# The up stage of a ConvFFN in seven products: halves cut at whole blocks, halo columns in four of the seven, and the second half of the first two tiles moved to the end

## The chip, the cores and the metric

The kernel runs on one core of a Trainium2 chip. A core has five engines with queues of their own: PE (matrix products, with PEld for its weight loads), DVE (vector), ACT (scalar functions), POOL (a second vector engine) and SP, which here only issues DMA transfers. They meet through semaphores. The metric is the device time of one launch in microseconds (us), the median of several runs. The kernel before takes 1351.69 us.

## The reference

One decoder layer for one sequence of 1024 tokens, with 16 meta tokens ahead of it and a width of 1024:

```
a = rmsnorm(h, ln_mix_pre);  proj = a @ w_in
y = concat(diff_attention(...), hgrn2(...))          # both read proj
h = h + rmsnorm(y @ w_out, ln_mix_post)
a = rmsnorm(h, ln_ffn_pre)
u = causal depthwise conv of width 3 over tokens (a @ w_up) + bias     # 1024 -> 2 * 2816
y = (gelu(u[:, :2816]) * u[:, 2816:]) @ w_down                         # 2816 -> 1024
h = h + rmsnorm(y, ln_ffn_post)                       # meta tokens dropped
```

All of it is fp32. The change lies between the output projection (`@ w_out`) and the down projection (`@ w_down`), in the product `a @ w_up`, called the up stage here.

## The kernel before, in words

A product in fp32 is made of three matmuls on split operands: every matrix is written as a high part (a cast) plus a low part (the rest, by a subtraction), and hi·hi, hi·lo and lo·hi are summed in PSUM. For the weights the cast is ACT's (`uh`) and the subtraction DVE's or POOL's (`ul`); for the activations ACT casts and DVE subtracts (`t`, in `t_split`).

**Output projection.** Tokens come in nine blocks: block 0 holds two meta tokens, blocks 1 to 8 hold 128 tokens each. Per block, SP loads the mixed heads (`mp`), PE projects, `post_a` and `post_b` do the norm and the residual (`xh`), and the FFN's normed input (`a2s`) comes out. `trans` turns a finished block by PE transposes and ACT copies it into `at2`, which holds `a2s` transposed: features on partitions, tokens along the free axis. At some blocks the loop also issues work for the up stage: `prep_plain` loads the weights of feature tile 0 and splits them, `t_split` splits quarters of `at2`.

**Up stage.** Output features come in 22 gate and 22 up tiles of 128; a feature tile here is the pair. The tokens are cut in two halves (`p` = 0 and 1), and each half in two columns of 258 (half 0) or 256 (half 1). The two more columns per half are the halo of the convolution: half 0 covers 516 columns, half 1 covers 512 from column 514 on, so that two columns are computed twice, and the convolution gives 514 and 510. For one feature tile and one half, gate and up, two quarters of the inner dimension and two columns make a 2x2 block product. `plain_unit` computes it with eight block products (96 matmuls); `unit` uses the Strassen-Winograd scheme: seven products of 12 matmuls, on sums of weight quarters (`w_sum` on POOL, `prep`) and sums of activation quarters (`t_sums` on DVE, in place in `at2`). In `unit`, products 0 and 4 go to bank `pa`, products 1, 3 and 5 to `pb`, products 2 and 6 to `pc`. Between them DVE adds the banks: `u2` is read from `pb` after product 1, and product 3 may go on in `pb` only then; `u3` is read after product 3, and `uu`, `ug` are the results. `conv` does the convolution (one ACT step and two DVE steps, `c0` for the gate and `c1` for the up side), `gated` the gelu on ACT and the product on POOL, and SP stores it to DRAM (`gsc`).

Feature tile 0 is done by `plain_unit`, half 0 and then half 1, so that PE has work before the sums of `at2` exist; tiles 1 to 21 follow with `unit`, both halves of a product one behind the other, so that a product is two groups of 12 matmuls. While a tile runs, the weights of the next are loaded and split (`prep(7 * (ft + 1) + j)` at step `j`).

**Down stage.** It reads `gsc` back (`gi`, split into `gh` on ACT and `gl` on DVE) and its own weights (`wi`, into `wh` and `wl`). A part of its first loads and splits is already issued in the up stage.

**Order.** PE's order is set by hand. On the other engines a scheduler orders the instructions ahead of time, and each engine works through its list strictly in that order: an instruction that waits holds up all behind it on that engine. The three lists shown with the change are such lists.

## Time and profile before

| what | before |
| --- | --- |
| median of 3 runs (lowest to highest) | 1351.69 us (1351.08 to 1352.4) |
| the profiled execution | 1352.21 us |
| its span, first to last instruction | 1350.4 us |
| mean granted TensorE clock | 0.991 |
| busy: PE / DVE / ACT / POOL | 1293.5 / 923.6 / 688.0 / 421.1 us |
| first matmul of the up stage | 661.7 us |
| first matmul of feature tile 1 | 694.7 us |
| first matmul of the down stage | 1128.25 us |

Rows of groups give line, engine, operation, names (out<-in), shapes, count, then busy time and mean duration of one, then the idle time of that engine just before and who ended it. L53 is the line of a helper through which all DVE and ACT operations go, so there one goes by the names. Rows of the timeline give start, length, engine and instruction. Rows of stretches give for each engine the busy time and the count of instructions in it.

### The profile page before, as it was taken

The numbers are of one execution on the slowest core, as the hardware profiler recorded it, in microseconds if no ns is written. First come the engines' busy times: TensorE is split into PE (matmuls) and PEld (weight loads), VectorE is DVE, ScalarE is ACT, GpSimd is POOL, SyncE is SP. The second block draws the span as 40 slices with busy tenths as digits, with TensorE's granted clock in tenths as the row PEclk, the third lists the DMA queues.
The fourth block names the chain that finished last, engine by engine and source line by source line (L and its number), as shares of the span: only waits on it lengthen the run. The fifth ranks groups of instructions, "written<-read, shape, count | busy, mean of one in ns | idle before, by whom it ended". The sixth has DMA issues, their size and how long they took to land.

```text
span 1350.4 us, 26183 instructions
## 1 busy us (share of the span) xinstructions
PE 1293.5 (96%) x10170; PEld 1194.3 (88%) x10170; DVE 923.6 (68%) x1597; ACT 688.0 (51%) x1625; POOL 421.1 (31%) x330
## 2 busy tenths in 40 slices
PE   6999999999999998999888999999999999999997
PEld 5898999989998998777688999999999998888885
DVE  7565657574747465736897777777877876597586
ACT  7365346535654565446674444544444444554454
POOL 3211211021112110111556656666566641010021
PEclk9999999999999999999999999999999999999999
DMA  6331232133211004626612222223222225965353
GB/s 213 106 131 53 103 125 103 44 127 102 102 37 48 19 29 121 209 78 213 232 40 87 94 71 71 94 71 108 89 71 74 92 72 171 343 211 159 100 202 117
DMA packets 84082, 153.06 MB, mean 113 GB/s; under 512 B 9539, under 2 KB 22627, under 8 KB 83958
## 3 DMA queue, kind: packets, MB, share of 16 engines
q1 hardware_dynamic: 83958, 151.39, 33.7%
q8 instruction: 80, 1.31, 0.4%
q14 instruction: 44, 0.36, 0.1%
HBM read 112.69 MB, written 38.67 MB: 112 GB/s over the span
## 4 chain that ended last, share of the span: by engine, by line
PE 68%; DVE 8%; ACT 4%; DMA 3%; issue 3%; POOL 1%; SPq 1%; DVEq 0%; ACTq 0%; POOLq 0%
PE pd L1449 5%; PE pd L1450 5%; PE pd L1448 5%; PE pb L1289 4%; PE pb L1290 4%; PE pb L1291 4%; PE pa L1289 3%; PE pa L1290 3%; PE pa L1291 3%; PE pc L1289 3%; PE pc L1291 3%; PE pc L1290 3%; PE pa L704 2%; PE py L964 2%; PE py L968 2%
## 5 line engine op out<-in xcount | busy, mean ns | idle before, releaser
L1289 PE MATMUL pb<-t,uh 128*128 128x258 f32 x504 | 144.4, 286 | 8.0 <-DVE u L53 8.0
L1290 PE MATMUL pb<-t,uh 128*128 128x258 f32 x504 | 143.4, 285 | 0.0
L1291 PE MATMUL pb<-t,ul 128*128 128x258 f32 x504 | 143.0, 284 | 0.0
L1449 PE MATMUL pd<-wl,gh 128*128 128x512 f32 x308 | 121.1, 393 | 0.5 <-DVE wl L53 0.5
L1450 PE MATMUL pd<-wh,gl 128*128 128x512 f32 x308 | 121.2, 393 | 0.0
L1448 PE MATMUL pd<-wh,gh 128*128 128x512 f32 x308 | 119.7, 388 | 0.0
L53 DVE SCALAR_TENSOR_TENSOR c<-uu,cwt,c 128x514 f32<-128x514 f32 (+1 forms) x88 | 96.3, 1095 | 20.6 <-ACT c L53 19.9
L1289 PEld LDWEIGHTS pb<-t,uh 128*128 128x128 f32 x504 | 96.3, 191 | 9.4 <-DVE u L53 8.8
L1256 POOL TENSOR_TENSOR c<-c,c 128x514 f32<-128x514 f32 (+1 forms) x44 | 63.4, 1441 | 121.9 <-ACT c L53 117.8
L1290 PEld LDWEIGHTS pb<-t,uh 128*128 128x128 f32 x504 | 96.9, 192 | 0.0
L1291 PEld LDWEIGHTS pb<-t,ul 128*128 128x128 f32 x504 | 96.7, 192 | 0.0
L1289 PE MATMUL pc<-t,uh 128*128 128x258 f32 (+1 forms) x336 | 95.1, 283 | 0.0
L1289 PE MATMUL pa<-t,uh 128*128 128x258 f32 (+1 forms) x336 | 94.7, 282 | 0.0
L1290 PE MATMUL pa<-t,uh 128*128 128x258 f32 (+1 forms) x336 | 94.7, 282 | 0.0
L1291 PE MATMUL pc<-t,ul 128*128 128x258 f32 (+1 forms) x336 | 94.5, 281 | 0.0
L1290 PE MATMUL pc<-t,uh 128*128 128x258 f32 (+1 forms) x336 | 94.5, 281 | 0.0
L1291 PE MATMUL pa<-t,ul 128*128 128x258 f32 (+1 forms) x336 | 94.4, 281 | 0.0
L53 DVE SCALAR_TENSOR_TENSOR c<-ug,cwt,c 128x514 f32<-128x514 f32 (+1 forms) x88 | 86.1, 978 | 2.6 <-ACT c L53 2.0
L155 POOL TENSOR_TENSOR ul<-ws,uh 128x512 fp32r<-128x512 f32 x42 | 59.9, 1427 | 48.2 <-ACT uh L53 44.0
L1449 PEld LDWEIGHTS pd<-wl,gh 128*128 128x128 f32 x308 | 57.8, 188 | 14.8 <-DVE wl L53 1.7
L53 ACT CAST uh<-ra 128x512 fp32r<-128x512 f32 x67 | 41.2, 616 | 56.1 <-PE pb L1290 36.2
L1448 PEld LDWEIGHTS pd<-wh,gh 128*128 128x128 f32 x308 | 57.8, 188 | 13.0
(394 smaller groups left out, 4162.8 us busy)
## 6 DMA issues: line engine op xcount, KB each, us to landing
ra<-in_wup_dram SPq DMA_DIRECT2D x88, 256.0 KB, 2.7
wd<-in_wdown_dram SPq DMA_DIRECT2D x44, 256.0 KB, 4.6
tsc<-wd SPq DMA_DIRECT2D x44, 256.0 KB, 3.2
...
```

Source lines behind the costliest of these rows:

```text
L53: ins = call(*args, **kw)
L155: (eng or G).tensor_tensor(lo, raw, hi.bitcast(F32), op=ALU.subtract)
L704: T.matmul(po[:, :P], w_, vn[:, j], start=(j == 0), stop=(j == i))
L964: T.matmul(py[:r], mh[:, j, :r], hi, start=(first and j == 0), stop=False)
L968: T.matmul(py[:r], ml[:, j, :r], hi, start=False, stop=(last and k == k1 - 1))
L1256: G.tensor_tensor(cg, cg, cu, op=ALU.mult)
L1289: T.matmul(pt, hi[:, s], th[:, k], start=(first and k == 0), stop=False, skip_group_check=True)
L1290: T.matmul(pt, hi[:, s], tl[:, k], start=False, stop=False, skip_group_check=True)
L1291: T.matmul(pt, lo[:, s], th[:, k], start=False, stop=(k == 3), skip_group_check=True)
L1448: T.matmul(py, gh[:, s], wh, start=(k == 0 and pr not in (3, 7)), stop=False, skip_group_check=True)
L1449: T.matmul(py, gh[:, s], wl, start=False, stop=False, skip_group_check=True)
L1450: T.matmul(py, gl[:, s], wh, start=False, stop=(k == NH - 1), skip_group_check=True)
```

## The change

**Halves.** Both halves now have 2 x 256 columns of whole blocks (`HALF`), and half 0 has two more at its left (`EDGE`): the two halo tokens of block 0. So no block straddles the halves, and `trans` has one ACT copy for each half of a block's features where a straddling block had two. The two halo columns lie only in the left column of half 0, and thus in products 0, 1, 4 and 5; products 2, 3 and 6 have 256 columns in both halves. Half 1 has no halo: `conv` copies the last two columns of the half before to the left edge of `ug` and `uu` (two small ACT copies per feature tile), and every convolution has 512 columns.

**Order of tiles.** `PLAN` lists the slots: only half 0 of tile 0 is done by `plain_unit`; then half 0 of tile 1 alone (slot 0); tiles 2 to 21 with both halves (slots 1 to 20); and at the end half 1 of tile 0 (slot 21) and of tile 1 (slot 22), for which the weights are loaded, summed and split once more, with all low parts on DVE. Names in the up stage now carry the slot: `u2_1_0` is slot 1, half 0, and belongs to tile 2, `u2_21_1` is slot 21, half 1. The outputs carry the tile (`uu21_1`).

**Earlier.** `prep_plain` is issued ahead of the projection's loop (it was at block 6), `prep(0)` and two splits at block 5, two more at block 6, the sums of half 0 at block 7. Block 8's transposes and the splits and sums of half 1 are issued step by step in slot 0 (`second`).

**Addresses.** The convolution's buffers lie elsewhere, padding tiles have other sizes, the two pools for split weights change parity, and the early steps of the down stage are taken in another order of k.

```diff
-WN = [258, 256]
-C0 = [0, 514]
+HALF = 256
+EDGE = [2, 0]
...
-        where.tile([P, n], F32, tag="lineup", name=f"lineup{len(lined)}", bufs=1)
+        where.tile([P, n], F32, tag=f"lineup{len(lined)}", name=f"lineup{len(lined)}", bufs=1)
...
+    line_up(ep, 48)
...
-        at2.append(a2p.tile([P, KD, 2 * WN[p]], F32, tag=f"at2_{p}", name=f"at2_{p}"))
+        at2.append(a2p.tile([P, KD, 2 * HALF + EDGE[p]], F32, tag=f"at2_{p}", name=f"at2_{p}"))
...
+        p, n = divmod(max(i - 1, 0), 4)
+        c = EDGE[p] + P * n if i else 0
...
-                        at2[p][:, ks, lo_ - C0[p]:hi_ - C0[p]], pv[:, :, lo_ - cs.start:hi_ - cs.start])
+            A.copy(at2[p][:, 4 * half:4 * half + 4, c:c + r], pt[:, : 4 * r].rearrange("p (k t) -> p k t", k=4))
...
+    def width(p, j):
+        return HALF + (EDGE[p] if j in (0, 1, 4, 5) else 0)
+
+    def t_split(p, j, src, where, tag, step=None):
+        n = width(p, j)
+        step = step or n
+        both = where.tile([P, 8, step], F32R, tag=tag, name=f"t{p}_{j}")
+        hi, lo = both[:, 0:4, :n], both[:, 4:8, :n]
+        o = n - src.shape[-1]
+        A.copy(hi[:, :, o:], src)
+        V.tensor_tensor(lo[:, :, o:], src, hi[:, :, o:].bitcast(F32), op=ALU.subtract)
+        if o:
+            for a, b in zip((hi, lo), tt[p][0]):
+                A.copy(a[:, :, :o], b[:, :, :o].bitcast(F32))
         tt[p][j] = (hi, lo)
...
+    def t_sums(p):
...
-        t_split(p, 1, b22, where, f"t{p}_1")
-        t_split(p, 2, b11, where, f"t{p}_2")
-        t_split(p, 3, b12, where, f"t{p}_3")
         V.tensor_tensor(b21, b21, b22, op=ALU.subtract)
-        t_split(p, 5, b21, *last)
...
+        if EDGE[p]:
+            e1, e2 = (at2[p][:, k0:k0 + 4, :EDGE[p]] for k0 in (0, 4))
+            V.tensor_tensor(e2, e2, e1, op=ALU.subtract)
...
+    PLAN = [(1, (0,))] + [(ft, (0, 1)) for ft in range(2, NF)] + [(0, (1,)), (1, (1,))]
...
-        ft, j = divmod(q, 7)
-        if ft >= NF:
+        s, j = divmod(q, 7)
+        if s >= len(PLAN):
...
-            load_raw4(ft)
+            load_raw4(PLAN[s][0], s)
...
-        where = swp if q % 2 else wp
+        where = wp if q % 2 else swp
...
-        split(hi, lo, src, G if j % 2 == 0 and j else V)
+        split(hi, lo, src, G if j % 2 == 0 and j and s < len(PLAN) - 2 else V)
...
+    prep_plain()
...
+        if i == 5:
+            prep(0)
+            t_split(0, 0, quarter(0, 0), ep, "e0")
+            t_split(0, 4, quarter(0, 4), ep, "e1")
         if i == 6:
-            prep_plain()
-        if i == 8:
             t_split(0, 7, quarter(0, 7), mxp, "mix0", 272)
             t_split(0, 6, quarter(0, 6), mxp, "mix1", 384)
+        if i == 7:
+            t_sums(0)
         post_a(i, py)
-        if i == 4:
-            t_split(0, 0, quarter(0, 0), ep, "e0")
-            t_split(0, 4, quarter(0, 4), ep, "e1")
     post_b(8)
...
-    line_up(xup, 16)
+    line_up(xup, 8)
+    v_cm, cv = pool("conv", 2)
...
+    edges = xup.tile([P, 2, 2, 2], F32, tag="edges", name="edges", bufs=1)
...
     def conv(ft, p, side, u):
         m = ft + NF * side
-        w = 2 * WN[p] - 2
-        c = cv.tile([P, 514], F32, tag=f"c{side}", name=f"c{side}_{ft}_{p}", bufs=2 if side else 3)[:, :w]
+        w = 2 * HALF
+        if p:
+            A.copy(u[:, :2], edges[:, ft, side] if ft < 2 else last[side][:, w:])
+        else:
+            last[side] = u
+            if ft < 2:
+                A.copy(edges[:, ft, side], u[:, w:])
+        c = cv.tile([P, w], F32, tag=f"c{side}", name=f"c{side}_{ft}_{p}", bufs=2 if side else 3)
...
-        SY.dma_start(gsc[P * ft: P * (ft + 1), C0[p]:C0[p] + 2 * WN[p] - 2], cg)
...
+        SY.dma_start(gsc[P * ft: P * (ft + 1), 2 * HALF * p:2 * HALF * (p + 1)], cg)
...
+    def plain_unit(bank):
+        us = outputs(0, 0)
         for col in range(2):
+            a = 0 if col == 0 else 2 + HALF
+            n = HALF + (2 if col == 0 else 0)
...
-    def unit(ft, p, bank):
-        n = WN[p]
...
+    def unit(s_, p, bank):
+        ft = PLAN[s_][0]
...
-            hi, lo = made[7 * ft + j]
+            hi, lo = made[7 * s_ + j]
             th, tl = tt[p][j]
+            pt = pt[:, HALF + e - width(p, j):]
...
+        V.tensor_tensor(u2, pb[:, e:], x1[:, e:], op=ALU.add)
...
+        V.tensor_tensor(u3, pb[:, e:], x1[:, e:], op=ALU.add)
+        V.tensor_tensor(uu[:, 2 + HALF:], pc[:, e:], u3, op=ALU.add)
...
+        A.copy(ug[:, 2 - e:2 + HALF], pa)
...
+        V.tensor_tensor(ug[:, 2 + HALF:], pc[:, e:], u2, op=ALU.add)
         gated(ft, p, ug, uu)
...
-    p0 = plain_unit(0, lambda nm: free.pop(0))
+    p0 = plain_unit(lambda nm: free.pop(0))
     next(p0)
     trans(7)
-    t_split(1, 0, quarter(1, 0), tp, "t1_0")
-    t_split(1, 4, quarter(1, 4), tp, "t1_4")
-    for _ in range(3):
-        next(p0)
-    trans(8)
-    t_split(1, 7, quarter(1, 7), tp, "t1_5")
-    t_split(1, 6, quarter(1, 6), mxp, "mix2", 384)
-    t_sums(0, tp, (mxp, "mix0", 272))
+    t_split(0, 1, sum_quarter(0, 1), tp, "t0_1", 264)
+    prep(1)
+    next(p0)
+    t_split(0, 2, sum_quarter(0, 2), tp, "t0_2")
+    next(p0)
+    prep(2)
+    t_split(0, 3, sum_quarter(0, 3), tp, "t0_3")
+    next(p0)
+    t_split(0, 5, sum_quarter(0, 5), mxp, "mix0", 272)
...
+    for j in range(3, 7):
+        prep(j)
...
-    p1 = plain_unit(1, ps_b)
-    for j in range(4):
-        prep(7 + j)
-        next(p1)
-    t_sums(1, t2p, (tp, "t1_5"))
-    close(a_cms.pop())
-    v_cm, cv = pool("conv", 2, "right")
-    line_up(cv, 8)
-    dn_cm, dn = pool("down", 4, "right")
-    next(p0)
-    for j in range(4, 7):
-        prep(7 + j)
-    for ft in range(1, NF):
-        units = [unit(ft, p, ps_b) for p in range(2)]
+
+    def second():
+        trans(8, ps_b)
+        yield
+        t_split(1, 0, quarter(1, 0), tp, "t1_0")
+        t_split(1, 4, quarter(1, 4), tp, "t1_4")
+        yield
+        t_split(1, 6, quarter(1, 6), mxp, "mix2", 384)
+        next(p0)
+        yield
+        t_sums(1)
+        yield
+        t_split(1, 1, sum_quarter(1, 1), t2p, "t1_1")
+        t_split(1, 2, sum_quarter(1, 2), t2p, "t1_2")
+        yield
+        t_split(1, 3, sum_quarter(1, 3), t2p, "t1_3")
+        t_split(1, 5, sum_quarter(1, 5), tp, "t1_5")
+        yield
+
+    p1_ops = second()
+    for s_, (_, ps) in enumerate(PLAN):
+        units = [unit(s_, p, ps_b) for p in ps]
         for j in range(7):
-            prep(7 * (ft + 1) + j)
+            prep(7 * (s_ + 1) + j)
             for u in units:
                 next(u)
-            if (ft, j) == (1, 1):
-                with tc.issue_after(marks[1, 1].ins):
-                    next(p1)
-    close(t2_cm, t_cm, xu_cm, mx_cm)
+            if s_ == 0:
+                next(p1_ops, None)
+        if s_ == 0:
+            close(a_cms.pop())
+            dn_cm, dn = pool("down", 4, "right")
...
-    for k in range(NH):
-        early.setdefault(min(3 + 3 * k, 2 * NH - 3 + k), []).append(k)
+    for n, k in enumerate((*range(2, 8), 0, 1, *range(8, NH))):
+        early.setdefault(min(3 + 3 * n, 2 * NH - 3 + k), []).append(k)
```

How this moves instructions is shown at three places. The first is SP's list near the end of the output projection (`mp8_0` to `mp8_3` are block 8's loads, `ra0_..` a weight quarter of feature tile 0 before and of slot 0, which is tile 1, in the change; slot 0's loads and those of the plain unit have like names). Before:

```order
L1145 DMA ra0_11_7584<-in_wup_dram 128x512
L1061 DMA xh7_7554<-in_x_dram 128x1024
L1145 DMA ra0_22_7586<-in_wup_dram 128x512
L1145 DMA ra0_21_7588<-in_wup_dram 128x512
L1145 DMA ra0_12_7590<-in_wup_dram 128x512
L1002 DMA mp8_0_7630<-msc_94 128x512
L1002 DMA mp8_1_7638<-msc_94 128x512
L1087 DMA hsc_91<-xh6_7487 128x1024
L1002 DMA mp8_2_7667<-msc_94 128x512
L1002 DMA mp8_3_7672<-msc_94 128x2x128
```

In the change:

```order
L1147 DMA ra0_11_7536<-in_wup_dram 128x512
L1062 DMA xh6_7506<-in_x_dram 128x1024
L1147 DMA ra0_22_7538<-in_wup_dram 128x512
L1147 DMA ra0_21_7540<-in_wup_dram 128x512
L1147 DMA ra0_12_7542<-in_wup_dram 128x512
L1002 DMA mp7_0_7578<-msc_94 128x512
L1002 DMA mp7_1_7586<-msc_94 128x512
L1088 DMA hsc_91<-xh5_7439 128x1024
L1002 DMA mp7_2_7613<-msc_94 128x512
L1002 DMA mp7_3_7618<-msc_94 128x2x128
```

Four weight loads and one x load stand in front of block 7's loads, where they stood in front of block 8's. The loads of the plain unit are now far ahead of these rows.

The second is DVE's list around the first `u2` of the first tile with two halves. Before, in tile 1 (`t` splits are long done):

```order
L53 SCALAR_TENSOR_TENSOR c0_0_0_8089<-ug0_0_7767,cwt_88,c0_0_0_8089 128x514
L53 SCALAR_TENSOR_TENSOR c1_0_0_8094<-uu0_0_7768,cwt_88,c1_0_0_8094 128x514
L53 TENSOR_TENSOR ul15_8169<-ws2_8166,uh15_8168 128x512
L53 TENSOR_TENSOR u2_1_0_8131<-pb1_0_8172,x1_1_0_8130 128x258
L53 TENSOR_TENSOR u2_1_1_8150<-pb1_1_8186,x1_1_1_8149 128x256
L53 SCALAR_TENSOR_TENSOR c0_0_1_8200<-ug0_1_7943,cwt_88,c0_0_1_8200 128x510
L53 SCALAR_TENSOR_TENSOR c1_0_1_8205<-uu0_1_7944,cwt_88,c1_0_1_8205 128x510
L53 SCALAR_TENSOR_TENSOR c0_0_1_8200<-ug0_1_7943,cwt_88,c0_0_1_8200 128x510
L53 SCALAR_TENSOR_TENSOR c1_0_1_8205<-uu0_1_7944,cwt_88,c1_0_1_8205 128x510
L53 TENSOR_TENSOR ul17_8244<-ws3_8241,uh17_8243 128x512
L53 TENSOR_TENSOR u3_1_0_8132<-pb1_0_8172,x1_1_0_8130 128x258
L53 TENSOR_TENSOR uu1_0_8129<-pc1_0_8215,u3_1_0_8132 128x258
```

In the change, in slots 0 and 1 (`t1_3`, `t1_5` are splits of half 1, `gl1_0` the first split of the down stage's input):

```order
L53 TENSOR_TENSOR t1_3_8123<-at2_1_7154,t1_3_8123 128x1024
L53 TENSOR_TENSOR t1_5_8126<-at2_1_7154,t1_5_8126 128x1024
L53 TENSOR_TENSOR ug1_0_7969<-pc0_0_8030,u2_0_0_7972 128x256
L53 SCALAR_TENSOR_TENSOR c1_1_0_8155<-uu1_0_7970,cwt_88,c1_1_0_8155 128x512
L53 TENSOR_TENSOR ul14_8176<-ra2_11_8165,uh14_8175 128x512
L53 SCALAR_TENSOR_TENSOR c0_1_0_8149<-ug1_0_7969,cwt_88,c0_1_0_8149 128x512
L53 SCALAR_TENSOR_TENSOR c1_1_0_8155<-uu1_0_7970,cwt_88,c1_1_0_8155 128x512
L53 SCALAR_TENSOR_TENSOR c0_1_0_8149<-ug1_0_7969,cwt_88,c0_1_0_8149 128x512
L53 TENSOR_TENSOR gl1_0_13777<-gi1_0_13772,gh1_0_13776 128x512
L53 TENSOR_TENSOR ul15_8220<-ws2_8217,uh15_8219 128x512
L53 TENSOR_TENSOR u2_1_0_8182<-pb1_0_8223,x1_1_0_8181 128x256
L53 TENSOR_TENSOR u2_1_1_8201<-pb1_1_8237,x1_1_1_8200 128x256
```

`u2_1_0` now stands behind two splits, four convolution steps and `gl1_0`; before, it stood behind four convolution steps, and `gl1_0` came after both `u3`.

The third is DVE's list at the end of the up stage. Before, where tile 21 is the last (`c0_20`, `c1_20` are the steps of tile 20, `wl1_0` a split of the down stage's weights):

```order
L53 TENSOR_TENSOR ug20_0_13155<-pc20_0_13231,u2_20_0_13158 128x258
L53 SCALAR_TENSOR_TENSOR c1_20_1_13399<-uu20_1_13175,cwt_88,c1_20_1_13399 128x510 x2
L53 SCALAR_TENSOR_TENSOR c0_20_0_13370<-ug20_0_13155,cwt_88,c0_20_0_13370 128x514
L53 TENSOR_TENSOR wl1_0_13652<-wi1_0_13645,wh1_0_13651 128x512
L53 SCALAR_TENSOR_TENSOR c0_20_0_13370<-ug20_0_13155,cwt_88,c0_20_0_13370 128x514
L53 TENSOR_TENSOR ug20_1_13174<-pc20_1_13244,u2_20_1_13177 128x256
L53 SCALAR_TENSOR_TENSOR c0_20_1_13394<-ug20_1_13174,cwt_88,c0_20_1_13394 128x510
L53 TENSOR_TENSOR u2_21_0_13408<-pb21_0_13443,x1_21_0_13407 128x258
```

In the change, where the single slot 21 follows slot 20 (whose results are `ug21`, `uu21`):

```order
L53 TENSOR_TENSOR ug21_1_13252<-pc20_1_13322,u2_20_1_13255 128x256
L53 SCALAR_TENSOR_TENSOR c0_21_0_13448<-ug21_0_13233,cwt_88,c0_21_0_13448 128x512
L53 SCALAR_TENSOR_TENSOR c1_21_1_13479<-uu21_1_13253,cwt_88,c1_21_1_13479 128x512
L53 SCALAR_TENSOR_TENSOR c0_21_1_13473<-ug21_1_13252,cwt_88,c0_21_1_13473 128x512
L53 TENSOR_TENSOR ul154_13496<-ra22_11_13485,uh154_13495 128x512
L53 SCALAR_TENSOR_TENSOR c0_21_1_13473<-ug21_1_13252,cwt_88,c0_21_1_13473 128x512
L53 TENSOR_TENSOR ul155_13521<-ws2_13518,uh155_13520 128x512
L53 TENSOR_TENSOR u2_21_1_13502<-pb21_1_13524,x1_21_1_13501 128x256
L53 TENSOR_TENSOR ul156_13539<-ws1_13493,uh156_13538 128x512
L53 TENSOR_TENSOR ul157_13558<-ws3_13555,uh157_13557 128x512
L53 TENSOR_TENSOR u3_21_1_13503<-pb21_1_13524,x1_21_1_13501 128x256
```

`u2_21_1` follows the steps of tile 21 and two splits of weights; slot 21 has only half 1, so `pb` is wanted again after three groups of matmuls and not after six.

80 lines of the change are left out of this document (30 added, 50 removed).

## The prediction

> **What bounds the kernel now.** I read the page first, then a table by stretches of the span, then the waits of PE.
>
> ```profile
> span 1350.4 us, 26183 instructions
> PE 1293.5 (96%) x10170; PEld 1194.3 (88%) x10170; DVE 923.6 (68%) x1597; ACT 688.0 (51%) x1625; POOL 421.1 (31%) x330
> ```
>
> PE is busy for 96% of the span, so only matmuls that go, or the 57 us in which PE is idle, can pay. The change touches the stretch from the last blocks of the output projection to the end of the up stage. Below, each row is a stretch (its length, then busy time and instructions of PE, PEld, DVE, ACT, POOL, then the granted clock): the plain unit; feature tiles 1, 2, 3 and 4; tiles 5 to 18.
>
> ```profile
> 661.70:694.70 33.00, 26.56 (x210) 26.13 (x209) 33.00 (x27) 21.78 (x40) 13.16 (x8) 0.95 0.18 65
> 694.70:718.20 23.50, 20.54 (x170) 20.13 (x169) 19.02 (x23) 11.79 (x21) 18.67 (x10) 1.00 0.28 91
> 718.20:743.10 24.90, 21.64 (x171) 21.44 (x170) 18.95 (x29) 12.11 (x21) 14.89 (x11) 0.93 0.25 86
> 743.10:763.20 20.10, 20.10 (x171) 20.10 (x170) 15.76 (x23) 10.03 (x18) 12.28 (x9) 1.00 0.29 92
> 763.20:787.00 23.80, 22.05 (x172) 21.78 (x171) 17.00 (x27) 10.67 (x20) 14.26 (x10) 0.93 0.23 78
> 787.00:1068.00 281.00, 281.00 (x2354) 280.53 (x2353) 213.95 (x306) 133.14 (x238) 177.56 (x127) 1.00 0.25 84
> ```
>
> From 743 on a tile is PE's own 20.1 us, with the one exception of tile 4. In the first row DVE is busy 33.00 of 33.00 us: there DVE sets the pace and PE waits. All waits of PE from 598 to 1128 (total, times, longest):
>
> ```profile
> PE pb L1289 <- DVE u L53: 8.0, 4, 3.3
> PE pq L1270 <- ACT ug L53: 4.3, 1, 4.3
> PE py L964 <- DMA mp<-msc: 3.0, 1, 3.0
> PE pa L1098 <- DVE a2s L53: 2.5, 2, 2.2
> ```
>
> The matmuls that ended three of them (start, length, and in brackets the idle time before):
>
> ```profile
> 678.09 0.39 PE L1270 MATMUL pq<-t,uh 128*128 128x258 f32 x1 [4.26 <-ACT ug L53]
> 730.26 0.58 PE L1289 MATMUL pb<-t,uh 128*128 128x258 f32 x1 [3.26 <-DVE u L53]
> 779.55 0.39 PE L1289 MATMUL pb<-t,uh 128*128 128x258 f32 x1 [1.75 <-DVE u L53]
> ```
>
> Some waits cost more than their length. The next rows, in the columns of the table above, are 3.4 us around or behind these three and behind the first wait of tile 1.
>
> ```profile
> 678.70:682.11 3.41, 3.41 (x19) 3.41 (x18) 3.41 (x3) 3.16 (x4) 1.32 (x1) 0.50 0.00 0
> 729.90:733.31 3.41, 3.05 (x14) 3.05 (x15) 1.48 (x3) 1.06 (x3) 3.22 (x3) 0.50 0.43 151
> 781.10:784.51 3.41, 3.41 (x19) 3.41 (x18) 2.03 (x5) 1.62 (x3) 0.11 (x1) 0.50 0.46 154
> 703.40:706.80 3.40, 1.82 (x15) 1.78 (x15) 3.40 (x6) 1.66 (x3) 2.62 (x2) 1.00 0.55 174
> ```
>
> Behind the waits of 4.26, 3.26 and 1.75 us the clock stood at half for 3.41 us; in tile 1, with 23.50 - 20.54 = 2.96 us of waits in two pieces, it stayed full. One such window costs what a tile is busy beyond 20.1: 21.64 - 20.1 = 1.5 us and 22.05 - 20.1 = 1.9 us; I use 1.6.
>
> **The change part by part.**
>
> *Fewer matmuls.* A plain unit of 96 matmuls becomes seven products of 12, so 12 go. *Narrower ones.* Products 2, 3 and 6 of the first half lose two columns: 21 feature tiles, 63 groups of 12. The starts of three successive groups, wide, narrow, wide:
>
> ```profile
> 907.22 0.29 PE L1289 MATMUL pa<-t,uh 128*128 128x258 f32 x1
> 908.67 0.28 PE L1289 MATMUL pa<-t,uh 128*128 128x256 f32 x1
> 910.09 0.28 PE L1289 MATMUL pb<-t,uh 128*128 128x258 f32 x1
> ```
>
> A wide group takes 1.45 us, a narrow one 1.42, that is 118 ns a matmul. So 12 x 0.118 = **-1.4 us**, and 63 x 0.03 = **-1.9 us** (nothing if the pace hangs on another thing than the columns, so 0 to -1.9).
>
> *The earlier loads and splits in the output projection.* The 3.0 us wait for mp belongs to the projection's last block: its loads stand on SP behind the four weight loads for the plain unit and an x load. In the new order the four loads for tile 1 and an x load stand just so ahead of block 7's loads. The stall moves one block forward at the same price: 0, with 1 us on either side for the first blocks, whose x and gain loads now stand behind the plain unit's loads. The four casts of the plain weights run earlier on ACT, while PE works on the projection; without that cover each costs what the first row here says.
>
> ```profile
> L53 ACT CAST uh<-ra 128x512 fp32r<-128x512 f32 x67 | 41.2, 616 | 56.1 <-PE pb L1290 36.2
> L53 ACT CAST t<-at 128x1024 fp32r<-128x1024 f32 x8 | 8.2, 1051 | 6.4 <-DVE a2s L53 3.2 <-DVE at L53 3.2
> L53 ACT COPY uu<-pq 128x258 f32<-128x258 f32 x2 | 0.7, 371 | 0.9 <-PE pq L1272 0.9
> ```
>
> *The border.* Before, 661.7 to 743.1 holds waits of 4.3 + 2.5 + (8.0 - 1.75) = 13.0 us and two half-clock windows, 3.0: 16.0 us lost. After, I walk the listed orders. The transposes of block 7 wait for a2s as before (2.5). The third plain product waits for ACT's copy out of its bank; the cast ahead of that copy no longer waits for the last a2s, so what is left is one t cast, the copy and the end of the last matmul, 1.05 + 0.37 + 0.4 = 1.8. The first product of tile 1 waits for the last such copy behind a weight cast: 0.62 + 0.37 + 0.2 = 1.2.
>
> Then DVE decides. In tile 1 (one half now) DVE has its u2 two groups and one instruction after the tile's start S, at S + 3.3; PE wants the next u2, that of tile 2, 13 groups after S, at S + 18.6, since tile 2 has two halves and six groups ahead of product 3. Between the two, DVE has 23 instructions in its order: five t subtractions, three sums in at2, six convolution steps, four ul, one gl and four u, uu or ug. Their durations before, contended and not:
>
> ```profile
> L53 DVE TENSOR_TENSOR t<-at,t 128x1024 fp32r<-128x1024 f32 x8 | 11.7, 1478 | 0.0
> L53 DVE TENSOR_TENSOR at<-at 128x1032 f32<-128x1032 f32 x3 | 5.9, 1955 | 0.0
> L53 DVE TENSOR_TENSOR at<-at 128x1024 f32<-128x1024 f32 x4 | 4.8, 1206 | 0.0
> L53 DVE SCALAR_TENSOR_TENSOR c<-ug,cwt,c 128x514 f32<-128x514 f32 x26 | 19.4, 747 | 0.0
> L53 DVE SCALAR_TENSOR_TENSOR c<-uu,cwt,c 128x514 f32<-128x514 f32 x6 | 6.9, 1157 | 1.9 <-ACT c L53 1.9
> L53 DVE TENSOR_TENSOR ul<-ws,uh 128x512 fp32r<-128x512 f32 x4 | 2.9, 719 | 0.5 <-ACT uh L53 0.5
> L53 DVE TENSOR_TENSOR u<-pb,x 128x258 f32<-128x258 f32 x4 | 1.7, 414 | 0.0
> ```
>
> With t and the sums at 1.2 and the steps at 0.75 that is 6.0 + 3.6 + 4.5 + 2.8 + 0.7 + 1.7 = 19.3 us; with t at 1.48, the sums at 1.5 (the mean of all seven) and the steps at 1.1 it is 23.7. DVE has 18.6 - 3.3 = 15.3 us, so PE loses 4.0 to 8.4 us here. I take the middle, 6.2, in two waits (about 2 in tile 1 and 4 in tile 2), the second with a window of 1.6. The sum after is 2.5 + 1.8 + 1.2 + 6.2 + 1.6 = 13.3, against 16.0: **-2.7 us** (-6.5 with the low end and no window, +1.1 with the high end and two).
>
> That a wait near 2 us can bring a window is shown by the 1.75 us one. The Trainium skill (TensorE: Matmul & The Clock Gate, Part 1, What's actually happening) gives half rate only after an idle window of about 3.4 us, in a free-running count. The windows' length and rate agree with the rows, the threshold does not: by it only the wait of 4.26 us would have brought one. By the page the upper end of this term would be 1.6 lower.
>
> *Tile 4.* Its wait of 1.75 for a u on DVE and its window of 1.9 stand alone among steady tiles. The second stage's early loads fall elsewhere in the order now. I see neither that the wait stays nor that it goes: half, **-1.8 us** (0 to -3.65).
>
> *The end.* Two slots of one half (tiles 0 and 1) now follow tile 21. Let T be the end of tile 21's matmuls. In a slot with one half PE wants u2 after three groups, at T + 3 x 1.42 = T + 4.3. Ahead of that u2 DVE has, as now, the convolution steps of the tile before. How they stand today, with T = 907.22:
>
> ```profile
> 910.86 0.42 DVE L53 TENSOR_TENSOR ug<-pc,u 128x256 f32<-128x256 f32 x1
> 911.20 0.75 DVE L53 SCALAR_TENSOR_TENSOR c<-ug,cwt,c 128x514 f32<-128x514 f32 x1
> 911.86 0.68 DVE L53 TENSOR_TENSOR ul<-ra,uh 128x512 fp32r<-128x512 f32 x1
> 912.46 2.44 DVE L53 SCALAR_TENSOR_TENSOR c<-ug,cwt,c 128x510 f32<-128x510 f32 x2
> 914.82 0.68 DVE L53 TENSOR_TENSOR ul<-ws,uh 128x512 fp32r<-128x512 f32 x1
> 915.43 0.74 DVE L53 TENSOR_TENSOR u<-pb,x 128x258 f32<-128x258 f32 x2
> ```
>
> The first u2 ends at T + 8.6, and two halves want it at T + 6 x 1.43 = T + 8.6: just in time, with no slack. The new order has one step more behind ug and the same two ul, so T + 9.4 at this pace; if POOL, with fewer subtractions there, leaves DVE steps of 0.75 us, it is T + 7.3. The first single slot thus stalls 3.0 to 5.1 us; I take 4.2, near the middle, and 1.6 for the window. The second slot has two steps between ug and u2, four in all and not eight, and comes in time. The cover that is gone is the other half's three groups. **+5.8 us** (+3.0 without a window, +7.0 at the high ends). The splits of the down stage's first weights stand ahead in DVE's order, so its start costs 0.
>
> *Edge copies.* Two ACT copies of two columns per tile: ACT is busy 133 of 281 us in the steady stretch, so 0. If they held u back, DVE's missing slack would pass it on, at up to the 0.37 us of a wide copy per tile; I leave that to the slow side.
>
> **Sum**: -1.4 - 1.9 - 2.7 - 1.8 + 5.8 = -2.0. The profiled execution took 1352.21 us (span 1350.4 and 1.8 around it), so 1350.2; it lies 0.5 above the median, so **1349.7**.
>
> **The rivals.**
>
> 1. *DVE keeps up at the border* (faster). With the border at its low end (-6.5), tile 4's wait gone (-3.65) and the end at 3.0 + 1.6: -1.4 - 1.9 - 6.5 - 3.65 + 4.6 = -8.9, so 1342.8. For it: the plain second half, whose work crowded the first row of the table, is gone from there. Against it: the splits of the second half are still there, and must still come before tile 2.
>
> 2. *DVE waits in its order for the second stage's transfer* (slower). The first gl now stands ahead of tile 2's u2, where before it stood behind both u3 of its tile. What it can cost stands here:
>
> ```profile
> 717.14 0.69 DVE L53 TENSOR_TENSOR gl<-gi,gh 128x512 fp32r<-128x512 f32 x1 [3.53 <-ACT gh L53]
> ```
>
> If those 3.5 us fall on u2, with DVE at the high end, the border loses 2.5 + 1.8 + 1.2 + 8.4 + 3.5 + 1.6 = 19.0 (+3.0), and tile 4's wait returns: -1.4 - 1.9 + 3.0 + 0 + 5.8 = +5.5, so 1357.2. It decides from a wait of about 3 us on. Against it: by the sum above DVE comes to this gl some 13 us after the last convolution step of the half that it reads.
>
> 3. *The width gives nothing*: 0 in place of -1.9, so 1351.6.
>
> **How the numbers follow.** What this kernel's runs can tell from no change is about 0.2%, 2.7 us: faster is below 1349.0, slower above 1354.4. Forecast: 0.36, own range 1346.5 to 1353, of which 0.15 lies below 1349 and 0.21 within. Rival 1: 0.25, all faster. Rival 2, with whatever of the end or the edge copies is worse than I take it: 0.29, of which 0.02 within. Rival 3: 0.10, of which 0.08 within and 0.02 above. Faster 0.15 + 0.25 = 0.40; same 0.21 + 0.02 + 0.08 = 0.31; slower 0.27 + 0.02 = 0.29. The range reaches from just below rival 1 to just above rival 2: 1342 to 1358.
>
> **What would show it.** In the new profile: one PE wait of about 3 us for mp, now before block 7; PE waits before pb of tiles 1 and 2 on DVE of 4 to 9 us together; no 4.26 us wait for ACT's ug; a PE wait of 3 to 5 us at pb of the first single slot, some 20 us ahead of the down stage; groups of 1.42 us for products 2, 3 and 6 in both halves. The forecast is wrong if u2 of that slot is read before PE wants it, if steady tiles take over 20.1 us again and again, or if the projection's blocks before 7 stall.

## The result and the profile after

The change makes the kernel slower: 1361.5 us, the median of five executions (1357.27 to 1364.46), against 1351.69 (1351.08 to 1354.07). The ratio, estimated from all executions and not from the two medians, is 1.0064, with a 95% interval of 1.0041 to 1.0088. In a second set of five, timed beside the experiments, it was 1358.31 us, ratio 1.0059 [1.0039, 1.0079]. The forecast was 1349.7 with a range up to 1358: wrong in sign, and outside the range. One disturbed execution of a later kernel (4417.78 us, the new halves in the old order) is left out of its ratio below.

The page of the change, to be held against the one of before:

```profile
span 1362.6 us, 26302 instructions
PE 1295.1 (95%) x10158; PEld 1193.2 (88%) x10158; DVE 933.1 (68%) x1616; ACT 700.0 (51%) x1684; POOL 432.7 (32%) x338
```

The 12 matmuls are gone, and yet PE is busy 1.6 us longer and idle 67.5 us in place of 57. This is the slowest of the five executions (1364.46 us), so the second profile, 1359.33 us with a span of 1357.5, is read beside it. The table by stretches, in the columns of the prediction: up to the first plain matmul; the plain half; slots 0 and 1 (tiles 1 and 2); tiles 3, 4 and 5; tiles 6 to 21; slot 21; slot 22; the down stage.

```profile
560.00:667.10 107.10, 100.64 (x583) 77.04 (x584) 64.56 (x95) 55.02 (x161) 28.82 (x19) 0.97 0.55 177
667.10:686.20 19.10, 14.36 (x106) 13.75 (x104) 14.44 (x15) 15.28 (x34) 3.53 (x4) 0.91 0.16 56
686.20:704.80 18.60, 13.15 (x93) 12.94 (x94) 16.20 (x14) 12.26 (x20) 15.40 (x9) 0.82 0.18 58
704.80:732.80 28.00, 22.54 (x171) 22.33 (x170) 21.50 (x28) 10.82 (x21) 13.29 (x10) 0.88 0.23 76
732.80:752.80 20.00, 19.96 (x171) 19.76 (x169) 14.98 (x23) 9.41 (x20) 11.72 (x9) 1.00 0.30 93
752.80:774.20 21.40, 20.29 (x171) 19.89 (x170) 15.79 (x24) 10.05 (x21) 13.04 (x10) 1.00 0.26 87
774.20:795.00 20.80, 20.13 (x171) 19.93 (x170) 16.04 (x24) 10.45 (x20) 14.34 (x11) 1.00 0.23 77
795.00:1112.70 317.70, 317.70 (x2691) 317.46 (x2690) 245.18 (x356) 157.48 (x305) 201.14 (x142) 1.00 0.25 84
1112.70:1127.80 15.10, 11.66 (x86) 11.46 (x85) 13.17 (x19) 7.95 (x19) 5.51 (x4) 0.89 0.30 91
1127.80:1137.70 9.90, 9.90 (x86) 9.90 (x85) 7.32 (x14) 5.36 (x10) 1.29 (x1) 1.00 0.37 127
1137.70:1362.60 224.90, 215.33 (x926) 174.03 (x924) 160.57 (x237) 107.52 (x217) 24.77 (x16) 0.99 0.58 190
```

A ledger follows from the starts of the first matmuls of each stretch. The second halves of tiles 0 and 1 are 21.4 us of matmuls before (180 of some 0.119 us); they are taken out of the border there and set against slots 21 and 22 (25.0 us). Differences to before, in us:

| stretch | predicted | measured | second profile |
| --- | --- | --- | --- |
| up to the first plain matmul (661.7, now 667.1; 665.0) | 0 | +5.4 | +3.3 |
| border, to the end of tile 2 (81.4 - 21.4 = 60.0, now 65.7; 65.8) | -2.7 | +5.7 | +5.8 |
| tiles 3 to 21 (385.15, now 379.9; 379.6) | -1.9 - 1.8 = -3.7 | -5.2 | -5.5 |
| second halves of tiles 0 and 1 (21.4, now 25.0; 24.8) | -1.4 + 5.8 = +4.4 | +3.6 | +3.4 |
| down stage (222.15, now 224.9; 222.2) | 0 | +2.75 | +0.1 |
| sum | -2.0 | +12.2 | +7.1 |

The border is the row on which the sign turned. All waits of PE from 560 to 1140 us of the change (total, times, longest):

```profile
PE pb L1307 <- DVE u L53: 16.1, 6, 5.5
PE pa L1100 <- DVE a2s L53: 5.5, 3, 2.8
PE py L964 <- DMA mp<-msc: 3.3, 1, 3.3
PE pq L1285 <- ACT ug L53: 1.4, 1, 1.4
PE pa L1307 <- ACT uu L53: 1.0, 1, 1.0
```

The matmuls that ended the long ones, two in the border and one at the end, and the one before them at block 7's transposes (start, length, and in brackets the idle time before):

```profile
672.52 1.16 PE L1100 MATMUL pa<-ident,a2s 128*128 128x128 f32 x8 [2.37 <-DVE a2s L53]
...
699.96 0.58 PE L1307 MATMUL pb<-t,uh 128*128 128x258 f32 x1 [5.45 <-DVE u L53]
...
718.88 0.58 PE L1307 MATMUL pb<-t,uh 128*128 128x256 f32 x1 [5.46 <-DVE u L53]
...
1120.52 0.57 PE L1307 MATMUL pb<-t,uh 128*128 128x256 f32 x1 [3.44 <-DVE u L53]
```

Behind each of the four came a stretch of half clock (the column after the five engines). Behind the two waits for a `u` in the border it lasted longer than one window of 3.41 us:

```profile
673.42:676.84 3.42, 3.42 (x18) 3.42 (x17) 3.42 (x5) 3.39 (x7) 0.00 (x0) 0.50 0.34 134
699.96:704.15 4.19, 4.19 (x19) 4.19 (x20) 4.19 (x4) 1.79 (x4) 3.64 (x3) 0.50 0.28 97
718.88:724.63 5.75, 5.75 (x27) 5.75 (x28) 2.37 (x5) 0.63 (x2) 3.71 (x3) 0.50 0.16 58
1120.50:1123.90 3.40, 3.38 (x16) 3.38 (x17) 2.62 (x3) 0.64 (x2) 2.65 (x2) 0.51 0.45 158
```

In these stretches the matmuls start some 0.214 us apart (seven steps from 719.47 to 720.97), and 0.118 at full clock, so each us of half clock costs some 0.45 us.

Why DVE was late shows in its own list. DVE between `uu` of tile 1 and the first `u2` of tile 2:

```profile
713.21 0.74 DVE L53 SCALAR_TENSOR_TENSOR c<-ug,cwt,c 128x512 f32<-128x512 f32 x1
713.87 1.75 DVE L53 SCALAR_TENSOR_TENSOR c<-uu,cwt,c 128x512 f32<-128x512 f32 x1
715.54 1.74 DVE L53 SCALAR_TENSOR_TENSOR c<-ug,cwt,c 128x512 f32<-128x512 f32 x1
717.21 0.68 DVE L53 TENSOR_TENSOR gl<-gi,gh 128x512 fp32r<-128x512 f32 x1
```

and POOL at the same time:

```profile
713.55 1.52 POOL L155 TENSOR_TENSOR ul<-ws,uh 128x512 fp32r<-128x512 f32 x1 [6.16 <-ACT uh L53]
715.15 1.59 POOL L1151 TENSOR_TENSOR ws<-ra,ws 128x512 f32<-128x512 f32 x1
```

The same step takes 0.74 us while POOL is idle (6.16 us up to 713.55) and 1.75 while POOL works. Over the whole trace, of the 176 convolution steps on DVE, the 89 that overlap less than 0.4 us of POOL's work have a median of 0.75 us, the other 87 one of 1.45. Between the two `u2`, from 691.10 to 718.41, DVE needed 27.3 us for the 23 instructions that were priced at 19.3 to 23.7.

### The profile page after: what moved, and what is told of

Same layout as the page of the kernel before. It is cut to its first block, busy times and chain, and to the rows that moved or that the text cites. A ratio compares the mean times of both kernels' runs of the same rounds, so it can differ in the third digit from the quotient of the medians.

```text
span 1362.6 us, 26302 instructions
## 1 busy us (share of the span) xinstructions
PE 1295.1 (95%) x10158; PEld 1193.2 (88%) x10158; DVE 933.1 (68%) x1616; ACT 700.0 (51%) x1684; POOL 432.7 (32%) x338
## 4 chain that ended last, share of the span: by engine, by line
PE 67%; DVE 9%; ACT 5%; DMA 3%; issue 3%; POOL 1%; SPq 1%; DVEq 0%; ACTq 0%; POOLq 0%
PE pd L1480 5%; PE pd L1481 5%; PE pd L1479 5%; PE pb L1307 4%; PE pb L1308 4%; PE pb L1309 4%; PE pa L1307 3%; PE pa L1308 3%; PE pa L1309 2%; PE pc L1307 2%; PE pc L1308 2%; PE pc L1309 2%; PE pa L704 2%; PE py L964 2%; PE py L968 1%
## 5 line engine op out<-in xcount | busy, mean ns | idle before, releaser
L1307 PE MATMUL pb<-t,uh 128*128 128x256 f32 (+1 forms) x516 | 148.7, 288 | 16.2 <-DVE u L53 16.1
L1309 PE MATMUL pb<-t,ul 128*128 128x256 f32 (+1 forms) x516 | 147.1, 285 | 0.0
L1308 PE MATMUL pb<-t,uh 128*128 128x256 f32 (+1 forms) x516 | 147.0, 285 | 0.0
L53 DVE SCALAR_TENSOR_TENSOR c<-uu,cwt,c 128x512 f32<-128x512 f32 x88 | 97.1, 1104 | 19.6 <-ACT c L53 18.8
L1270 POOL TENSOR_TENSOR c<-c,c 128x512 f32<-128x512 f32 x44 | 64.6, 1469 | 120.8 <-ACT c L53 112.8
L1307 PE MATMUL pa<-t,uh 128*128 128x256 f32 (+1 forms) x344 | 97.4, 283 | 1.0 <-ACT uu L53 1.0
L1308 PE MATMUL pa<-t,uh 128*128 128x256 f32 (+1 forms) x344 | 96.9, 282 | 0.0
L1307 PE MATMUL pc<-t,uh 128*128 128x256 f32 x344 | 96.9, 282 | 0.0
L1308 PE MATMUL pc<-t,uh 128*128 128x256 f32 x344 | 96.8, 281 | 0.0
L1309 PE MATMUL pc<-t,ul 128*128 128x256 f32 x344 | 96.8, 281 | 0.0
L1309 PE MATMUL pa<-t,ul 128*128 128x256 f32 (+1 forms) x344 | 96.6, 281 | 0.0
L53 DVE SCALAR_TENSOR_TENSOR c<-ug,cwt,c 128x512 f32<-128x512 f32 x88 | 85.0, 966 | 3.7 <-ACT c L53 3.0
L1151 POOL TENSOR_TENSOR ws<-ra,ra 128x512 f32<-128x512 f32 x46 | 69.0, 1499 | 9.8 <-DVE ul L53 4.1
L1480 PEld LDWEIGHTS pd<-wl,gh 128*128 128x128 f32 x308 | 58.1, 189 | 14.4 <-DVE wl L53 1.1
```

Of the source, the lines that this page charges most:

```text
L53: ins = call(*args, **kw)
L1151: G.tensor_tensor(sums[nm], a, b, op=op)
L1270: G.tensor_tensor(cg, cg, cu, op=ALU.mult)
L1307: T.matmul(pt, hi[:, s], th[:, k], start=(first and k == 0), stop=False, skip_group_check=True)
L1308: T.matmul(pt, hi[:, s], tl[:, k], start=False, stop=False, skip_group_check=True)
L1309: T.matmul(pt, lo[:, s], th[:, k], start=False, stop=(k == 3), skip_group_check=True)
```

## The experiments

Each is compared with the kernel before on the same chip; times are medians.

**The change once more**, for what differs from one execution to the next.

> The changed kernel once more, to see which of its waits repeat. Theory A (DVE's order and its slow instructions while POOL works set the waits): PE waits again for a2s ahead of block 6's transposes (2.8 us before), twice about 5.5 us for u in tiles 1 and 2, about 3.4 us in slot 21; time 1357 to 1364. Theory B (the waits come from transfers that were late in that one execution): these waits change by more than 1 us each.

1358.31 us, 1.0059 [1.0039, 1.0079]. The border (65.8), the tiles and the end agree with the first profile within 0.3 us: the two long waits for a `u` are there again (11.4 us together, 10.9 before), and so is the 3.44 us in slot 21. The start and the down stage do not agree (last column of the ledger): the wait at block 6's transposes is 0.62 us and not 2.83. So about 5 of the 12 us of the first profile are not the change's in every execution.

**The norm ahead of the splits**: in the projection's last blocks, DVE's and ACT's splits and sums are issued only behind the norm that ends in `a2s`.

```diff
-        if i == 6:
-            t_split(0, 7, quarter(0, 7), mxp, "mix0", 272)
-            t_split(0, 6, quarter(0, 6), mxp, "mix1", 384)
         if i == 7:
-            t_sums(0)
+            with tc.issue_after(normed[6].ins):
+                t_split(0, 7, quarter(0, 7), mxp, "mix0", 272)
+                t_split(0, 6, quarter(0, 6), mxp, "mix1", 384)
+                t_sums(0)
...
-    t_split(0, 1, sum_quarter(0, 1), tp, "t0_1", 264)
+    with tc.issue_after(normed[7].ins):
+        t_split(0, 1, sum_quarter(0, 1), tp, "t0_1", 264)
...
-        t_split(1, 0, quarter(1, 0), tp, "t1_0")
+        with tc.issue_after(normed[8].ins):
+            t_split(1, 0, quarter(1, 0), tp, "t1_0")
```

> The change, with the two splits and the sums of half 0 placed on DVE behind block 6's norm (a2s) instead of ahead of it. Theory A (these splits and sums hold up the norm): the 2.8 us wait ahead of block 6's transposes and the half clock behind it go, the first plain matmul starts 3 to 4.5 us earlier, near 662.5; up to 2 us come back later. Time 2 to 4.5 us under the change. Theory B (the norm is late because its x load stands behind four weight loads on SP): the wait stays over 2 us and the time stays within 1 us.

1362.86 us, 1.0091 [1.007, 1.0113]: no gain, but some 4.5 us more than the change in the same set (1358.31). The wait at block 6's transposes is gone, and one block on stand, in the lists of PE and DVE:

```profile
674.50 1.97 PE L1100 MATMUL pa<-ident,a2s 128*128 128x128 f32 x8 [6.76 <-DVE a2s L53]
```

```profile
672.56 0.69 DVE L53 TENSOR_TENSOR tmp<-py,gpo 128x512 f32<-128x512 f32 x1 [4.66 <-ACT at L53]
```

The splits that were held back come due there, and it is not DVE's share of them that holds up the norm: DVE stands idle for 4.66 us, while ACT makes the held-back casts ahead of the step of the norm that DVE waits for. How much of this wait is the edit's is not shown: with the order of the change, in the kernel with the parity put back, the same transposes waited 5.47 us.

**The last convolution later**: the convolution, gelu and product of tile 21 (both halves) are issued in slot 21, behind its second product.

```diff
-        gated(ft, p, ug, uu)
+        if s_ == len(PLAN) - 3:
+            held.append((ft, p, ug, uu))
+        else:
+            gated(ft, p, ug, uu)
...
+            if s_ == len(PLAN) - 2 and j == 1:
+                for h in held:
+                    gated(*h)
```

> The change, with the convolution of slot 20 issued only behind u2 of slot 21. Theory A (u2 is late because it stands behind the convolution steps): the 3.4 us wait in slot 21 falls to 0 to 2 us, and slots 21 and 22 together take 20.5 to 23 us where they took 25.0. Time 2 to 4.5 us under the change. Theory B (u2 waits for its operands on ACT or for weights): slots 21 and 22 still take 24.5 us or more.

1357.73 us, 1.005 [1.003, 1.007], beside 1358.31 for the change: no difference that could be measured. Its two end slots:

```profile
1107.50:1119.00 11.50, 10.59 (x87) 9.99 (x86) 11.50 (x18) 6.68 (x17) 5.69 (x4) 1.00 0.20 70
1119.00:1131.00 12.00, 10.00 (x87) 9.84 (x86) 8.11 (x15) 6.43 (x11) 2.27 (x2) 1.00 0.43 153
```

Slot 21 falls from 15.0 to 11.5 us, without half clock; slot 22 grows from 9.9 to 12.0 by a new wait of 2.00 us for a `u`. Together 23.5 against 24.8: the stall is real, and 1.3 us of it can be had in this way, which lies between the two theories.

**Addresses in the down stage**: the buffers of `gh` and `gl` (four each) are claimed ahead of those of `gi`, so they lie elsewhere in the pool.

```diff
+            for tag, kind in (("gh", F32R), ("gl", F32R)):
+                for n in range(4):
+                    dn.tile([P, 512], kind, tag=tag, name=f"{tag}first{n}")
```

> The change, with the down stage's gh, gl and gi buffers in another order in their pool: gh at the address 138880, where before it stood at 136832 and in the change at 147072. Theory A (the pace of the down stage's matmuls hangs on where its operands lie): the mean start-to-start pace falls from 233.2 to about 230 ns and the down stage from 224.9 to about 222 us; time about 2.7 us under the change. Theory B (the pace was slower through that execution's clock or through the other order of k): it stays at 233 ns.

1358.02 us, 1.0057 [1.0038, 1.0076]. The down stage took 222.25 us, as short as before's, but so it was in the second profile of the change, with no address moved. The other addresses are not shown to matter.

**Parity of the weight pools put back** (one execution).

```diff
-        where = wp if q % 2 else swp
+        where = swp if q % 2 else wp
```

> The change, with the two pools of split weights swapped back to the parity of before, so that every product's weights lie where the other parity's lay. Theory A (where the weights and the activations lie has no part in the pace): steady tiles of 19.85 us again. Theory B (it has): steady tiles differ by 0.1 us or more.

1359.33 us; steady tiles take 19.85 us again. The parity has no part in the gain of the steady tiles.

**Narrower products alone**: before, with products 3 and 6 of half 0 at 256 columns (their two halo columns are left out).

```diff
+            if p == 0 and j in (3, 6):
+                pt, th, tl = pt[:, :256], th[:, :, :256], tl[:, :, :256]
```

> The kernel before, with products 3 and 6 of half 0 computed on 256 columns instead of 258 (two halo columns are left without these two products); every address and every other instruction is as before. Theory A (a matmul costs its columns, 2.5 ns for two): 21 x 24 x 2.5 ns = 1.3 us less, steady tiles 0.06 us shorter. Theory B (the steady tiles of the change are shorter for another reason than the columns): tiles stay within 0.02 us of 20.03 and 20.20. Theory C (a group whose width differs from its neighbour's has another pace): 0.1 us or more per tile.

1348.37 us, 0.9985 [0.9969, 1.0001]. Tiles 5 to 18 of this kernel:

```profile
787.80:1066.90 279.10, 279.10 (x2355) 279.10 (x2354) 210.60 (x306) 133.68 (x238) 178.48 (x127) 1.00 0.24 84
```

14 tiles in 279.1 us are 19.94 us each, against 281.0 / 14 = 20.07 before; the change has 317.7 / 16 = 19.86. So 24 narrowed matmuls bring 0.13 us a tile and 36 bring 0.21, that is 5.6 and 5.9 ns each, and not the 2.5 of the prediction.

**POOL's work of slots 0 to 2 left out** (one execution): the sums of weight quarters that POOL makes there are not made, and the low parts that it splits are replaced by the high ones; DVE has the same list.

```diff
+        if short:
+            sums[nm] = a
+            return a
...
+        if short and j % 2 == 0 and j:
+            A.copy(hi, src)
+            made[q] = (hi, hi)
+            return
```

> The change, with POOL's sums and subtractions for the weights of slots 0 to 2 left out (the products of these three slots use plain weights in place of sums, and the high part in place of four low parts); DVE's list is the same. Theory A (two-input instructions on DVE take up to twice as long while POOL works, and that is what makes u late): from u2 of slot 0 to u2 of slot 1 DVE takes 19 to 21 us instead of 27.3, and PE's waits for u in tiles 1 and 2 fall from 11 to 12 us together to 3 to 6. Theory B (DVE waits there for ACT and for transfers): 25 us or more, and waits of 10 us or more.

1342.48 us. DVE's groups of two SBUF operands in the border (mean ns behind the busy time), first in the change from 686.2 to 718.4 us,

```profile
L53 DVE TENSOR_TENSOR t<-at,t 128x1024 fp32r<-128x1024 f32 x5 | 8.1, 1653 | 0.0
L53 DVE TENSOR_TENSOR at<-at 128x1024 f32<-128x1024 f32 x4 | 7.5, 1868 | 2.4 <-ACT at L53 2.4
L53 DVE SCALAR_TENSOR_TENSOR c<-uu,cwt,c 128x512 f32<-128x512 f32 x4 | 6.0, 1496 | 0.0
L53 DVE TENSOR_TENSOR u<-pb,x 128x256 f32<-128x256 f32 x2 | 0.8, 414 | 0.0
```

then here, in the same place of the program (678.3 to 702):

```profile
L53 DVE TENSOR_TENSOR at<-at 128x1024 f32<-128x1024 f32 x4 | 5.9, 1484 | 2.4 <-ACT at L53 2.4
L53 DVE TENSOR_TENSOR t<-at,t 128x1024 fp32r<-128x1024 f32 x5 | 5.9, 1213 | 0.0
L53 DVE SCALAR_TENSOR_TENSOR c<-uu,cwt,c 128x512 f32<-128x512 f32 x4 | 3.0, 744 | 0.0
L53 DVE TENSOR_TENSOR u<-pb,x 128x256 f32<-128x256 f32 x4 | 1.6, 414 | 0.0
```

The steps fall from 1496 to 744 ns, the `t` from 1653 to 1213. The `at` fall less, because one of the four (at 687.71) still meets a POOL instruction (at 687.63) and takes 2.28 us; the other three take 1.21 to 1.23. The whole border:

```profile
659.10:713.50 54.40, 45.94 (x366) 44.72 (x365) 41.88 (x54) 37.14 (x72) 8.07 (x6) 0.97 0.25 87
```

54.4 us against 65.7: 11.3 of the 16 to 19 us that this kernel is shorter than the change; most of the rest lies ahead of the first plain matmul (659.1, not 667.1 or 665.0). From the first `u2` to the next DVE needs 18.5 us where it needed 27.3, just below the low end of the prediction's sum (19.3), and PE's waits for a `u` fall from 10.9 to 2.8 us. So with the same list on DVE the border is 5.6 us shorter than before's 60.0 when POOL is out of the way, and 5.7 longer with POOL's work beside it. The `u` additions, with one operand in PSUM, take 414 ns in both. This is what the Trainium skill says (SBUF — State Buffer, Who interferes with whom): a DVE instruction with two SBUF inputs contends with a GpSimd instruction that reads SBUF, one with at most one, outside the modes that use two ports, does not. The runs agree, and add the price.

**The new halves in the old order**: from before, with the whole blocks per half, the narrow products and the new addresses, but both halves of every tile together and the loads, splits and sums where they were (the diff is cut to the order).

```diff
+    PLAN = [(ft, (0, 1)) for ft in range(1, NF)]
...
-    for ft in range(1, NF):
-        units = [unit(ft, p, ps_b) for p in range(2)]
+    for s_, (_, ps) in enumerate(PLAN):
+        units = [unit(s_, p, ps_b) for p in ps]
         for j in range(7):
-            prep(7 * (ft + 1) + j)
+            prep(7 * (s_ + 1) + j)
```

> The change's halves (whole blocks, halo columns in four products, edge copies), but the order of before: the plain unit computes both halves of tile 0, tiles 1 to 21 follow with both halves, loads and splits in the output projection where they were before, k in its old order. Theory A (the loss comes from the order of the tiles: the second halves of tiles 0 and 1 were PE's cover while DVE splits half 1): from the first plain matmul to the end of tile 2 it takes 80 to 83 us (before 81.4), no wait at the end of the up stage, steady tiles of 19.85 us; time 1345 to 1348. Theory B (the loss comes from the new halves and the edge copies): the border loses 5 us or more against before, time 1353 or more.

1348.65 us, 0.9986 [0.9971, 1.0001]. No stall stands at its end, the steady tiles take 19.85 us, and from the first plain matmul to the end of tile 2 it takes 78.9 us, less than the 80 to 83 expected and than the 81.4 of before. What the change lost is gone; that something is left of a gain is likely, but the interval just reaches 1.

**The early part too**: the last kernel with the change's early loads, splits and sums in the projection.

```diff
+    prep_plain()
...
+        if i == 5:
+            prep(0)
+            t_split(0, 0, quarter(0, 0), ep, "e0")
+            t_split(0, 4, quarter(0, 4), ep, "e1")
         if i == 6:
-            prep_plain()
-        if i == 8:
...
+        if i == 7:
+            t_sums(0)
```

> The new halves in the order of before (as e7_old_order), but with the weight loads, splits and sums of half 0 issued early in the output projection, as in the change. It tells what this part of the change is worth by itself. Theory A (it only moves the 3 us wait for mp one block forward and DVE's work from the border into the projection): time within 2 us of e7_old_order. Theory B (with the cover of both plain halves the earlier sums pay): 3 us or more under e7_old_order.

1348.95 us, 0.9985 [0.9975, 0.9996], the same as without. It differs from the change in the order of the tiles and in what goes with it: the places of half 1's splits, of block 8's transposes and of tile 1's weight splits, and the order of k in the down stage's early steps, which is that of before. That makes 0.9985 against 1.0059, each against before on its own chip: 0.74% or 10 us. From its first plain matmul to the end of tile 2:

```profile
662.30:738.60 76.30, 66.50 (x545) 65.05 (x544) 62.38 (x70) 45.01 (x92) 35.94 (x23) 0.98 0.21 73
```

76.3 us (78.9 without the early part), with the second halves of tiles 0 and 1 in it. The change needs 65.7 there and 25.0 at the end, 90.7 in all. Some 3 us of these 14.4 come back in tiles 3 to 5, and 2.7 in the down stage, by the pace told of below.

**A bank of its own for the fourth plain product**, in the old order, so that it doesn't wait for ACT's copy.

```diff
-    both = ps_s("pq2")
-    free += [both[:, 0], both[:, 1]]
+    free += [ps_s("pq2")[:, 0], None]
...
-    p0 = plain_unit(0, lambda nm: free.pop(0))
+    p0 = plain_unit(0, lambda nm: free.pop(0) if len(free) > 1 else ps_m("pq3"))
```

> The new halves in the order of before (as e7_old_order), with the fourth plain product of half 0 in a PSUM bank of its own instead of the second bank of the third product's tile. Theory A (the 5.1 us wait of that product is for ACT's copy out of the shared tile): that wait goes, 3 to 4 us of it come back as a wait of block 8's transposes for a2s, and the first matmul of tile 1 starts 1 to 4 us earlier after the first plain matmul than the 34.5 us of e7_old_order. Time 1344 to 1347. Theory B (DVE is the bound of this stretch, so every wait removed comes back): 34 us or more again, time as e7_old_order, about 1348.6.

1349.56 us, 0.9993 [0.9983, 1.0003]. Plain unit and tile 1 here:

```profile
661.20:692.90 31.70, 26.35 (x209) 25.72 (x208) 31.66 (x26) 23.80 (x48) 13.82 (x7) 0.95 0.24 84
692.90:721.80 28.90, 23.32 (x170) 22.93 (x170) 23.70 (x25) 12.21 (x25) 18.48 (x12) 0.88 0.24 83
```

They take 31.7 + 28.9 us, and 34.5 + 24.3 without the bank: the plain unit gains 2.8 us, since a 5.1 us wait for ACT's copy is gone, and tile 1 loses 4.6, in waits for DVE and the half clock behind them. DVE is busy for 31.66 of the 31.70 us.

**Both**: early part and own bank.

> Both edits together: new halves, old order of the tiles, early loads and sums, own bank for the fourth plain product. Theory A (the edits add): 1 to 4 us under the better of the two. Theory B (DVE is the bound of the stretch): as the better of the two, within 1 us.

1347.87 us (1346.46 to 1349.65), 0.9982 [0.9973, 0.9992]: its interval and that of the early part alone are the only ones that exclude 1 on the fast side, and its ratio is the lowest of all kernels that leave nothing out. It beats the change by about 0.8%, and before by 0.2%, which is at the edge of what can be told. That the two edits add is not shown: it is 1.1 us under the better of the two.

## Why the prediction was wrong

**The step that failed** is the border: "The sum after is 2.5 + 1.8 + 1.2 + 6.2 + 1.6 = 13.3, against 16.0: -2.7 us". The walk through the lists was right: the waits stand where it put them, for the instructions it named. Its sizes were not. Of the waits, 2.37, 1.42 and 0.95 us came for 2.5, 1.8 and 1.2, but 5.45 + 5.46 = 10.9 for the 6.2 of DVE. And three stretches of half clock came for one, of 3.42, 4.19 and 5.75 us: 13.4 us at some 0.45 is 6.0 us for the 1.6. That is +4.0 and +4.4, the whole 8.4 us between -2.7 and +5.7.

The 6.2 was "the middle" between DVE durations with and without contention. The high end, 23.7 us, used means over the border of before, t at 1.48 and steps at 1.1. But those means mix contended and free instructions. With POOL busy for 15.4 of the 18.6 us of slot 0, the `at` went to 1.87 and `c<-uu` to 1.5, as means over slots 0 and 1. The bound from above was the contended instruction, and before's trace had it: there too 88 of 176 convolution steps meet POOL's work, with a median of 1.45 us against 0.75. The run without POOL's work shows the cause; that the order alone makes it show is seen in the kernel with the early part and the old order, where the same work of DVE and POOL is covered by 21.4 us more matmuls, and PE's longest wait for a `u` is 2.2 us. The prediction counted these matmuls as moved work at an even price, and nowhere as the cover that DVE's splits of half 1 have in the border. It said so itself of the end ("The cover that is gone is the other half's three groups") and not of the place that the halves were taken from.

**The end**: "+5.8 us". Slot 21 stalled 3.44 us (4.2 taken, range 3.0 to 5.1), with one stretch of half clock: it took 15.1 us, 5.2 more than slot 22. DVE's list before it, and POOL's at the time:

```profile
1117.78 1.75 DVE L53 SCALAR_TENSOR_TENSOR c<-ug,cwt,c 128x512 f32<-128x512 f32 x1
1119.46 0.68 DVE L53 TENSOR_TENSOR ul<-ws,uh 128x512 fp32r<-128x512 f32 x1
1120.06 0.41 DVE L53 TENSOR_TENSOR u<-pb,x 128x256 f32<-128x256 f32 x1
```

```profile
1116.72 2.26 POOL L1270 TENSOR_TENSOR c<-c,c 128x512 f32<-128x512 f32 x1 [3.66 <-ACT c L53]
```

`u2` comes at T + 7.4 (T = 1112.69), near the low end of T + 7.3, since of the five steps between only this one met POOL's work. The second slot is in time. Right.

**Fewer matmuls**, -1.4: slots 21 and 22 took 25.0 us in place of 21.4, and 25.0 - 21.4 - 5.2 = -1.6. Right.

**Width**, -1.9: right in sign, too small by more than half. At 5.9 ns for each of 756 matmuls it is -4.5 us. The row of three groups (1.45, 1.42 us) was taken as the price of two columns everywhere, but that price hangs on the product: in the run with narrower products alone, product 6 of half 0 fell from 120.8 to 113.9 ns a matmul, product 3 from 124.0 to 121.9, and product 2 of half 1, not narrowed and just ahead of product 3, from 120.9 to 118.6 (means over tiles 8 to 18). Rival 3 (nothing) falls.

**Tile 4**, -1.8: its wait of 1.75 us with its window is gone, but tiles 4 and 5 take 21.4 and 20.8 us, together 2.5 more than two steady tiles, where before tile 4 had 3.65 more. Between the ends, -1.2 for the -1.8 taken.

**The early part**, 0: the wait for `mp` moved one block forward at 3.3 us (3.0 before), and with and without the early part the old order took 0.9985 and 0.9986. Right, on the whole. The +5.4 us of the first profile's start is mostly a wait of 2.8 us at block 6's transposes with half clock behind it, one of the prediction's own signs of being wrong (a stall of the blocks before 7); in the second profile that wait is 0.6, and 2.6 of its 3.3 us are there before the projection's first matmul (532.94, before 530.35). It is not a fixed price of the change.

**Rival 1** (DVE keeps up) needed the low sum, which DVE reached only with POOL's work left out. **Rival 2** forecast 1357.2, near what came, by a mechanism that did not: in the list above `gl` runs at 717.21, straight behind the step before, with no wait for a transfer. Its place was right, the `u2` of tile 2; what was late there was DVE itself.
